# Up-projection of the channel mixer: block products chained in PSUM banks, three engines in a written-out order, GpSimd without elementwise work

## The chip, the cores and the metric

The kernel runs on one core of a Trainium2 chip. The metric is the device time of one launch in microseconds (us); the median of three runs is given. Engines: PE is TensorE (matmul), PEld its weight loads, DVE is VectorE, ACT is ScalarE, POOL is GpSimd, SP is SyncE, which here only issues DMAs.

## The reference, cut to what matters

Two layers of a decoder trunk (1024 tokens, 1024 channels, float32). Layer 0 mixes tokens by a short convolution and differential attention, layer 1 by RWKV-7. Behind each mixer stands the channel mixer, the only part that the change touches:

```python
def conv_glu_ffn(x, w_up, conv_w, conv_b, w_down):
    h = causal_dwconv(x @ w_up, conv_w) + conv_b     # 1024 -> 2 * 2816 columns; width-3 conv over tokens
    gate, up = jnp.split(h, 2, axis=-1)
    return (jax.nn.silu(gate) * up) @ w_down         # 2816 -> 1024
```

Products are float32 to nearly full precision: each operand is split into a high and a low part, and three matmuls (high by high, high by low, low by high) stand for one.

## The kernel before, in words

The up-projection takes the 5632 columns as 22 column tiles, c = 0 to 21; a tile is 128 gate columns and the 128 value columns that belong to them. As a 2 x 2 block product (columns by halves of the channels, times halves of the channels by halves of the tokens) a tile needs seven block products, by Winograd's form of Strassen's scheme. They are numbered 1 to 7 and written P1 to P7 below. Each is 4 x 3 = 12 matmuls of 128x128 by 128x512 (`mm3`, three lines in a row, called from `product`), so a tile is 84 matmuls.

Around the products of one tile stands elementwise work:

- Four sums of weight blocks, S1 to S4 (`block`, tile `ws`), on POOL in before. The weights `wr` come by two DMAs of 512 KB a tile (part 0 and part 1), issued by SP.
- For each product the split of its weight block (`prep`): a cast on ACT to the high part, a subtraction on DVE for the low part (both into tile `wu`), FLA = 5 products ahead.
- Sums of the products (`add`, on DVE, tiles `u`, `hv` and the PSUM tile `up`), and one copy on ACT.
- The convolution of the gate half and of the value half (`conv`): the first tap on ACT, the other two on DVE (tile `cv`), then SiLU on ACT and the product of gate and value, on POOL in before. The result `G` goes to DRAM by a DMA that POOL issues.

The generator `ffn` does one step for each product. Tiles 0 and 1 go side by side, product by product (14 steps); from then on (20 tiles, 140 steps) one tile follows the other. Their first steps run while the mixer's output projection ends, since the operands B11, B21, B22 and T1 to T4 (tiles `x`, `xt`) are made from the mixer's layer norm in `mixer_operands`; T3 and T4 are subtracted on POOL. `dn` is the down-projection that follows.

The order of each engine's queue is not the order of the code: the framework's scheduler sorts the instructions by priority and by its own estimate of times, and places semaphores. Each engine then takes its queue in order.

Of the kernel before, what the change touches and what calls it, by code (L numbers as in the profile page):

```python
# [13 lines left out]
ALU = mybir.AluOpType  # L14
# [16 lines left out]
FLA = 5  # L31
FILL = 3
# [31 lines left out]
class Kern:  # L64
# [73 lines left out]
    def mm3(self, ps, ah, al, bh, bl, first, last):  # L138
        nc = self.nc
        nc.tensor.matmul(ps, ah, bh, start=first, stop=False)  # L140
        nc.tensor.matmul(ps, ah, bl, start=False, stop=False)  # L141
        nc.tensor.matmul(ps, al, bh, start=False, stop=last)  # L142
# [41 lines left out]
    def mixer_operands(self, zs, half, gname, bname, xo):  # L184
        """the blocks B11, B21, B22 and sums T1 to T4 that the up-projection takes, in high and low parts"""
# [22 lines left out]
        for name, d, x, y in (("B22", None, None, None), ("T1", lo, (raw, lo), (old, lo)), ("T2", hi, (raw, hi), (ts, lo)),  # L208
                              ("T3", lo, (raw, hi), (raw, lo)), ("T4", hi, (ts, hi), (old, hi))):
# [8 lines left out]
    def ffn(self, l, xo, resid, tail, nxt=None):  # L218
        """generator, one step for each block product of the up-projection. That takes a gate tile and a value tile of
        128 columns together: as 2 x 2 blocks (columns by halves of the channels, times halves of the channels by  # L220
        halves of the tokens) they come from seven block products, by Winograd's form of Strassen's scheme."""
# [11 lines left out]
        def block(c, name):  # L233
            """a block of the weights, or a sum of such"""
# [17 lines left out]
        def prep(n):  # L252
            if n < len(seq):
# [3 lines left out]
                nc.scalar.copy(t[:, lo], src)  # L257
                nc.vector.tensor_sub(t[:, hi], src, t[:, lo].bitcast(F32))  # L258

        def conv(src, ct):  # L260
            cc = self.U("cv")
            nc.scalar.activation(cc, src, AF.Identity, bias=self.pc_(bname, ct), scale=self.pc_(wname, 88 + ct))  # L262
            nc.vector.scalar_tensor_tensor(cc[:, 1:], src[:, :T - 1], self.pc_(wname, 44 + ct), cc[:, 1:], ALU.mult, ALU.add)  # L263
            nc.vector.scalar_tensor_tensor(cc[:, 2:], src[:, :T - 2], self.pc_(wname, ct), cc[:, 2:], ALU.mult, ALU.add)  # L264
            return cc

        def product(c, i):
            w = W[c]
            xn = prods[i][1]
# [3 lines left out]
            t = w.pop(i)  # L273
            for j in range(4):
                k, x = j * P, xo[xn][j]
                self.mm3(ps, t[:, k:k + P], t[:, 512 + k:512 + k + P], x[:, lo], x[:, hi], j == 0, j == 3)
            add = nc.vector.tensor_add
# [7 lines left out]
            if i == 7:  # L285
# [4 lines left out]
                w["gate"] = True  # L290
            if i == 5:
                w["p5"] = ps
            if i in (3, 7) and "gate" in w and not any(k in w for k in (3, 7)):
                add(w["A"][:, hi], w["A"][:, hi], w["u"][:, hi])  # L294
                w["g"] = conv(w["A"], c)
                nc.scalar.activation(w["g"], w["g"], AF.Silu)
            if i == 4:
                nc.vector.tensor_sub(w["h"][:, lo], w["u"][:, lo], ps)
                v = conv(w["h"], NC + c)
                nc.gpsimd.tensor_tensor(v, w["g"], v, op=ALU.mult)  # L300
                nc.gpsimd.dma_start(GS[c], v)
                W[c].clear()
# [17 lines left out]
        for n, (c, i) in enumerate(seq):  # L320
            prep(n + FLA)
            product(c, i)
            if n == len(seq) - 3:
                operands(0, 0)
                operands(0, 1)
            yield
# [53 lines left out]
    def make_tail(self, gi, bi, row, mode):  # L380
        """gi, bi: parameter names; row: (g, b) DRAM rows. Returns (tail, result)."""
# [5 lines left out]
        def tail(t, r, dh):  # L387
            """goes on with half dh of a tile of tokens"""
# [50 lines left out]
    def out_proj(self, w, yhl, resid, tail, in_w=(0, 1, 7), eng=None):  # L439
        """generator: loads the weights, then goes on by tiles of 128 tokens"""  # L440
# [21 lines left out]
    def mixer0(self, then):  # L462
# [61 lines left out]
        # generators of filling work: each step is one half of a column tile of the input projection  # L524
# [51 lines left out]
        # attention, one tile of 128 queries of one head after the other  # L576
# [27 lines left out]
        def turn(hd, i, p):  # L604
            """the weights of one tile, keys first"""
# [54 lines left out]
        # operands of the output projection: the last head's come two tiles at a time  # L660
# [31 lines left out]
        # queries and keys of the first head follow the input as it arrives  # L692
# [68 lines left out]
    def rwkv(self, xf, then):  # L761
# [29 lines left out]
        def variant(i, kt, x=None, h=None, eng=None):  # L791
            """x plus its mixed difference to the token before: of all tokens, or of one half of them"""
# [8 lines left out]
        def ahead(items, make, n=2):  # L801
            """items with what make gives for them, n of these in the making before one is used"""
# [16 lines left out]
        def spread(xs, i, src=None):  # L819
            """generator: the operands of a projection"""  # L820
# [15 lines left out]
        def lora1(steps):  # L836
            """generator: the first products of several low-rank maps, over the channel tiles"""
# [104 lines left out]
        # receptance, with the loras between its tiles; its start fills the gap behind what comes before  # L942
# [33 lines left out]
        def gates():  # L976
            """generator: the gate, written out for later"""
# [28 lines left out]
        # second lora weights: high and low parts stacked against the doubled hidden rows  # L1006
# [605 lines left out]
```

## Time and profile before

| | us |
|---|---|
| median of three runs (lowest, highest) | 2854.09 (2852.14, 2866.19) |
| span of the profiled execution, the one time the page has for it | 2858.8 |
| PE busy, DVE busy, ACT busy, POOL busy | 2639.9, 2065.9, 1060.9, 850.0 |
| up-projection of layer 0: tiles 0 and 1, then tiles 2 to 21 | 537.9 to 603.2, 603.2 to 1010.3 |
| up-projection of layer 1: tiles 0 and 1, then tiles 2 to 21 | 2135.2 to 2198.2, 2198.2 to 2605.9 |

The stretches are read off the starts of the `up` matmuls: the 169th of a layer begins tile 2. The span is 4.7 us above the median run and lies between the lowest and the highest. Two things help in reading the rows. Instructions of one engine overlap a little in the records, so that what one costs is the distance to the next start, not its length. And a matmul's record is longer than its turn on PE for the same reason.

### The profile page before, as it was taken

What the parts mean: (1) busy time and instruction counts of PE and PEld (TensorE: products, weight loads), DVE (VectorE), ACT (ScalarE), POOL (GpSimd) and SP (SyncE); (2) the same over time, 40 slices, a digit from 0 to 9 for tenths busy, and PEclk for the clock granted to TensorE, in tenths of its full rate; (3) what the DMA queues carried; (4) which work ended last, traced back from release to release, by engine and by line L of the source; (5) the groups of instructions that cost most, each with busy time, mean ns of one, the idle gap of its engine ahead of it and who ended that gap; (6) DMA issues with size and microseconds to landing.
All of it is one profiled execution on the core that took longest, in us unless ns stands there. A gap on an engine that the chain in (4) does not pass through costs nothing. (4 is left out here: it accounts for less than half of the span.)

```text
span 2858.8 us, 38102 instructions
## 1 busy us (share of the span) xinstructions
PE 2639.9 (92%) x14736; PEld 2140.1 (75%) x14736; DVE 2065.9 (72%) x2796; ACT 1060.9 (37%) x1650; POOL 850.0 (30%) x558
## 2 busy tenths in 40 slices
PE   8999989979998999999998998688897999899998
PEld 6777777768777788777876777577776787778886
DVE  4645656699999964657778656777759999997463
ACT  3323343234343441526665223334224344334330
POOL 0000003564554303010045211345555455441000
PEclk9999979999999999999997998787998999999999
DMA  5111233122222173543256779777431222224751
GB/s 163 52 45 52 63 114 104 67 74 74 82 83 71 67 231 115 195 158 111 89 188 217 230 219 232 175 175 204 154 125 48 93 78 78 82 74 158 240 187 41
DMA packets 208678, 358.10 MB, mean 125 GB/s; under 512 B 88945, under 2 KB 118257, under 8 KB 208497
## 3 DMA queue, kind: packets, MB, share of 16 engines
q1 hardware_dynamic: 198704, 320.01, 36.1%
q0 software_dynamic: 9792, 35.66, 3.4%
q8 instruction: 116, 1.90, 0.3%
q14 instruction: 66, 0.53, 0.1%
HBM read 255.46 MB, written 95.94 MB: 123 GB/s over the span
## 5 line engine op out<-in xcount | busy, mean ns | idle before, releaser
L140 PE MATMUL up<-x,wu 128*128 128x512 f32 x1232 | 485.3, 397 | 47.4 <-DVE u L282 22.4
L142 PE MATMUL up<-x,wu 128*128 128x512 f32 x1232 | 479.0, 397 | 10.3 <-DVE wu L258 10.2
L141 PE MATMUL up<-x,wu 128*128 128x512 f32 x1232 | 486.1, 395 | 0.8 <-DVE x L148 0.7
L140 PEld LDWEIGHTS up<-x,wu 128*128 128x128 f32 x1232 | 234.5, 191 | 106.4 <-DVE up L284 26.7
L142 PEld LDWEIGHTS up<-x,wu 128*128 128x128 f32 x1232 | 234.7, 191 | 69.7 <-DVE wu L258 21.0
L300 POOL TENSOR_TENSOR cv<-cv,cv 128x1024 f32<-128x1024 f32 x44 | 161.3, 3665 | 413.5 <-DVE cv L264 362.6
L141 PE MATMUL dn<-wdl,gt 128*128 128x512 f32 x704 | 274.5, 390 | 0.7 <-DVE wdl L118 0.7
L140 PE MATMUL dn<-wdh,gt 128*128 128x512 f32 x704 | 273.9, 390 | 0.2 <-ACT xf L182 0.2
L141 PEld LDWEIGHTS up<-x,wu 128*128 128x128 f32 x1232 | 235.2, 191 | 51.2 <-DVE x L148 3.1
L142 PE MATMUL dn<-wdh,gt 128*128 128x512 f32 x704 | 271.2, 390 | 0.0
L258 DVE TENSOR_TENSOR wu<-wr,wu 128x512 fp32r<-128x512 f32 x132 | 223.8, 1716 | 6.4 <-ACT wu L257 6.4
L258 DVE TENSOR_TENSOR wu<-ws,wu 128x512 fp32r<-128x512 f32 x176 | 221.9, 1264 | 0.2 <-ACT wu L257 0.2
L118 DVE TENSOR_TENSOR wdl<-raw,wdh 128x1024 fp32r<-128x1024 f32 x88 | 116.5, 1324 | 100.6 <-ACT wdh L117 91.6
L262 ACT ACTIVATE cv<-up,par 128x1024 f32<-128x1024 f32 x44 | 53.1, 1207 | 363.1 <-DVE up L294 363.1
L141 PE MATMUL pr<-xv,wph 128*128 128x512 f32 x384 | 155.2, 404 | 6.1 <-DVE xv L816 4.2
L140 PE MATMUL pj<-x,wih 128*128 128x512 f32 x384 | 152.8, 408 | 7.7 <-ACT x L147 7.6
L140 PE MATMUL pr<-xv,wph 128*128 128x512 f32 x384 | 154.2, 406 | 5.8 <-DVE kp L1057 4.3
L142 PE MATMUL pr<-xv,wpl 128*128 128x512 f32 x384 | 155.2, 404 | 4.2 <-DVE wpl L118 4.2
L117 ACT CAST wdh<-raw 128x1024 fp32r<-128x1024 f32 x88 | 92.6, 1052 | 173.6 <-DMA raw<-wdn 108.7
L141 PEld LDWEIGHTS dn<-wdl,gt 128*128 128x128 f32 x704 | 132.5, 188 | 28.6 <-DVE wdl L118 1.1
L140 PEld LDWEIGHTS dn<-wdh,gt 128*128 128x128 f32 x704 | 132.6, 188 | 27.8 <-ACT xf L182 0.4
L142 PE MATMUL pj<-x,wil 128*128 128x512 f32 x384 | 153.2, 399 | 0.2 <-DVE wil L118 0.2
(301 smaller groups left out, 5700.6 us busy)
## 6 DMA issues: line engine op xcount, KB each, us to landing
wr<-wup SPq DMA_DIRECT2D x88, 512.0 KB, 3.6
raw<-wdn SPq DMA_DIRECT2D x88, 512.0 KB, 3.8
G<-cv POOLq DMA_DIRECT2D x44, 512.0 KB, 3.0
gr<-G SPq DMA_DIRECT2D x88, 256.0 KB, 3.8
bk<-bkS SPq DMA_DIRECT2D x32, 512.0 KB, 6.3
spill<-acc SPq DMA_DIRECT2D x24, 512.0 KB, 2.6
res<-spill SPq DMA_DIRECT2D x24, 512.0 KB, 4.8
raw<-win SPq DMA_DIRECT2D x22, 512.0 KB, 3.7
```

The source lines that it names most:

```text
L117: self.nc.scalar.copy(hi, raw)
L118: self.nc.vector.tensor_sub(lo, raw, hi.bitcast(F32))
L140: nc.tensor.matmul(ps, ah, bh, start=first, stop=False)
L141: nc.tensor.matmul(ps, ah, bl, start=False, stop=False)
L142: nc.tensor.matmul(ps, al, bh, start=False, stop=last)
L258: nc.vector.tensor_sub(t[:, hi], src, t[:, lo].bitcast(F32))
L262: nc.scalar.activation(cc, src, AF.Identity, bias=self.pc_(bname, ct), scale=self.pc_(wname, 88 + ct))
L300: nc.gpsimd.tensor_tensor(v, w["g"], v, op=ALU.mult)
```

## The change

From the 15th step of `ffn` on (tiles 2 to 21), in both layers:

- The queues of PE, DVE and ACT are no longer sorted by the scheduler: a region (`manual_schedule`) keeps them in the order of the code. A step (slot) issues its product's 12 matmuls, the subtraction for the product four slots on, its share of the convolution, one sum of blocks for the next tile, the cast for the product five slots on, and then the addition that takes this product. SP and POOL stay with the scheduler.
- Products are in the order 1, 6, 2, 5, 7, 3, 4 (before 1, 6, 5, 2, 7, 3, 4) and are chained in PSUM: P2 adds onto P1's bank, P5 and P3 onto P6's, P4 onto P7's. Before, each had a bank of its own, and DVE added. A tile has five additions on DVE in place of seven, and three banks (a two-bank tile `A`, and `z`) in place of one for each product.
- The four sums S1 to S4 and the product of gate and value move from POOL to DVE. POOL keeps the DMA of `G`.
- The convolution of a tile is spread over the slots of this tile and the next.

For tiles 0 and 1 the steps stay as they were, under the scheduler, but for the product of gate and value, which moves to DVE as well, and for T4, whose sign is turned so that its product is added instead of subtracted. Docstrings and some comments are dropped, which shifts line numbers: L258 of before is L265, L249 is L250, L300 is L301 and L352, and L140 to L142 are L141 to L143. The core of the diff:

```diff
-                nc.gpsimd.tensor_tensor(w[name], x, y, op=op)
+                (nc.vector if c > 1 else nc.gpsimd).tensor_tensor(w[name], x, y, op=op)
...
+        def tap(cc, src, ct, k):
+            if k == 0:
+                nc.scalar.activation(cc, src, AF.Identity, bias=..., scale=...)
+            else:
+                nc.vector.scalar_tensor_tensor(cc[:, k:], src[:, :T - k], ..., cc[:, k:], ALU.mult, ALU.add)
...
-                nc.gpsimd.tensor_tensor(v, w["g"], v, op=ALU.mult)
+            nc.vector.tensor_tensor(v, w["g"], v, op=ALU.mult)
...
+        def late(c, i):
+            b = c - 1
+            if i == 4:
+                w = W[c]
+                w["g"] = self.U("cv")
+                tap(w["g"], w["A"], c, 0)
+                tap(w["g"], w["A"], c, 1)
+            elif b > 1:
+                w = W[b]
+                if i == 1:
+                    w["v"] = self.U("cv")
+                    tap(w["v"], w["h"], NC + b, 0)
+                    tap(w["g"], w["A"], b, 2)
+                elif i == 6:
+                    nc.scalar.activation(w["g"], w["g"], AF.Silu)
+                    tap(w["v"], w["h"], NC + b, 1)
+                elif i == 2:
+                    tap(w["v"], w["h"], NC + b, 2)
+                elif i == 5:
+                    nc.vector.tensor_tensor(w["v"], w["g"], w["v"], op=ALU.mult)
+                    nc.gpsimd.dma_start(GS[b], w["v"])
+                    w.clear()
+            name = {1: "S1", 2: "S2", 7: "S3", 3: "S4"}.get(i)
+            if name and c + 1 < NC:
+                block(c + 1, name)
+
+        def chained(n, c, i):
+            w = W[c]
+            if i == 1:
+                w["A"], w["u"] = self.A("up"), self.U("u2")
+            if i == 7:
+                w["z"] = self.B("up")
+            if i == 6:
+                nc.scalar.copy(w["u"][:, lo], w["A"][:, lo])
+            ps = w["z"] if i in (7, 4) else w["A"][:, lo if i in (1, 2) else hi]
+            multiply(c, i, ps, i in (1, 6, 7), skip_group_check=True)
+            sub(n + FLA - 1)
+            late(c, i)
+            cast(n + FLA)
+            if i == 6:
+                add(w["u"][:, hi], w["u"][:, lo], ps)
+            if i == 5:
+                w["h"] = self.U("hv")
+                add(w["h"][:, hi], w["u"][:, lo], ps)
+            if i == 7:
+                add(w["h"][:, hi], w["h"][:, hi], ps)
+            if i == 3:
+                add(ps, ps, w["u"][:, lo])
+            if i == 4:
+                add(w["h"][:, lo], w["u"][:, hi], ps)
...
-        seq += [(c, i) for c in range(2, NC) for i in (1, 6, 5, 2, 7, 3, 4)]
+        seq += [(c, i) for c in range(2, NC) for i in (1, 6, 2, 5, 7, 3, 4)]
...
+                if n == 14:
+                    region.enter_context(self.tc.manual_schedule(engines=ORDERED))
+                if n < 14:
+                    prep(n + FLA)
+                    apart(c, i)
+                else:
+                    chained(n, c, i)
```

What stands in DVE's queue before, for a stretch a little over half a tile long in the middle of layer 0 (L258 the subtractions of the split, L282 to L298 the additions, L263 and L264 the taps; `wr` and `ws` name the source of a subtraction):

```order
L258 TENSOR_TENSOR wu_974_5497<-ws_973_5494,wu_974_5497 128x512
L284 TENSOR_TENSOR up_975_5500<-up_975_5500,u2_966_5455 128x512
L258 TENSOR_TENSOR wu_976_5514<-ws_973_5494,wu_976_5514 128x512
L287 TENSOR_TENSOR u2_966_5455<-u2_966_5455,up_977_5517 128x512
L258 TENSOR_TENSOR wu_979_5534<-wr_969_5474,wu_979_5534 128x512
L288 TENSOR_TENSOR hv_978_5530<-u2_966_5455,up_972_5481 128x512
L289 TENSOR_TENSOR u2_966_5455<-u2_966_5455,up_972_5481 128x512
L298 TENSOR_TENSOR hv_978_5530<-u2_966_5455,up_983_5560 128x512
L294 TENSOR_TENSOR up_975_5500<-up_975_5500,u2_966_5455 128x512
L263 SCALAR_TENSOR_TENSOR cv_980_5550<-up_975_5500,par_81,cv_980_5550 128x1023
L263 SCALAR_TENSOR_TENSOR cv_984_5574<-hv_978_5530,par_81,cv_984_5574 128x1023
L264 SCALAR_TENSOR_TENSOR cv_980_5550<-up_975_5500,par_81,cv_980_5550 128x1022
```

The same queue now, from the slot of P1 of a tile on (L265 the subtractions, L250 the sums S1 to S4, L277 the taps, L352 gate by value, L374 and L377 the additions that take P6 and P5):

```order
L265 TENSOR_TENSOR wu_894_5012<-ws_883_4947,wu_894_5012 128x512
L277 SCALAR_TENSOR_TENSOR cv_890_5003<-hv_881_4931,par_81,cv_890_5003 128x1023
L374 TENSOR_TENSOR u2_889_4989<-u2_889_4989,up_888_4988 128x512
L265 TENSOR_TENSOR wu_895_5030<-wr_875_4872,wu_895_5030 128x512
L277 SCALAR_TENSOR_TENSOR cv_890_5003<-hv_881_4931,par_81,cv_890_5003 128x1022
L250 TENSOR_TENSOR ws_893_5010<-ws_893_5010,wr_891_5006 128x512
L265 TENSOR_TENSOR wu_896_5048<-wr_891_5006,wu_896_5048 128x512
L352 TENSOR_TENSOR cv_890_5003<-cv_886_4982,cv_890_5003 128x1024
L377 TENSOR_TENSOR hv_898_5067<-u2_889_4989,up_888_4988 128x512
L265 TENSOR_TENSOR wu_897_5065<-ws_893_5010,wu_897_5065 128x512
L250 TENSOR_TENSOR ws_900_5083<-wr_891_5006,wr_892_5008 128x512
L379 TENSOR_TENSOR hv_898_5067<-hv_898_5067,up_899_5069 128x512
```

One subtraction now stands in each slot, taps and additions alternate with them, and the sums and the product of gate and value have come over from POOL.

On SP, the loads of the weights `wr` in the middle of layer 0, before (part 0 and part 1 of a tile, then those of the next):

```order
L239 DMA wr_948_5332<-wup 128x1024
L239 DMA wr_949_5334<-wup 128x1024
L239 DMA wr_969_5474<-wup 128x1024
L239 DMA wr_970_5476<-wup 128x1024
L239 DMA wr_990_5616<-wup 128x1024
```

and now (part 0 of tile 7, part 1 of tile 6, part 0 of tile 8, part 1 of tile 7, part 0 of tile 9):

```order
L240 DMA wr_908_5142<-wup 128x1024
L240 DMA wr_892_5008<-wup 128x1024
L240 DMA wr_925_5278<-wup 128x1024
L240 DMA wr_909_5144<-wup 128x1024
L240 DMA wr_942_5414<-wup 128x1024
```

Part 1 of a tile now stands behind part 0 of the tile after it. A part 0 waits until the tile two before has given its buffer back, which its S4 on DVE does last.

On PE, the seam between P6 and the next product of tile 2, before (each product its own bank, `up_842`, then `up_846`):

```order
L140 MATMUL up_842_4608<-x_791_4321,wu_823_4486 128x512
L141 MATMUL up_842_4608<-x_791_4321,wu_823_4486 128x512
L142 MATMUL up_842_4608<-x_791_4321,wu_823_4486 128x512
L140 MATMUL up_846_4629<-x_784_4293,wu_827_4512 128x512
L141 MATMUL up_846_4629<-x_784_4293,wu_827_4512 128x512
```

and now (P6, then P2; both write the two-bank tile `up_838`, each one half):

```order
L141 MATMUL up_838_4588<-x_791_4321,wu_823_4486 128x512
L142 MATMUL up_838_4588<-x_791_4321,wu_823_4486 128x512
L143 MATMUL up_838_4588<-x_791_4321,wu_823_4486 128x512
L141 MATMUL up_838_4588<-x_700_3781,wu_827_4512 128x512
L142 MATMUL up_838_4588<-x_700_3781,wu_827_4512 128x512
```

P2 now writes onto the bank that holds P1, so it waits for ACT's copy of P1; likewise P5 waits for the addition that reads P6, P3 for the one that reads P5, and P4 for the one that reads P7.

## Rows read from the trace of the kernel before

**Rows 1.** Page, part 1: busy us (share of the span) and instructions.
```profile
PE 2639.9 (92%) x14736; PEld 2140.1 (75%) x14736; DVE 2065.9 (72%) x2796; ACT 1060.9 (37%) x1650; POOL 850.0 (30%) x558
```

**Rows 2.** Windows of the up-projections: stretch, length, busy us by engine, TensorE clock, DMA.
```profile
537.90:603.20 65.30, 47.33 (x202) 37.88 (x201) 55.98 (x64) 27.42 (x45) 45.88 (x22) 0.87 0.16 57
603.20:1010.30 407.10, 391.19 (x1682) 315.57 (x1681) 380.64 (x364) 157.88 (x224) 193.81 (x118) 0.99 0.24 82
2135.20:2198.20 63.00, 48.44 (x202) 37.52 (x201) 58.84 (x64) 25.78 (x43) 38.99 (x20) 0.86 0.14 51
2198.20:2605.90 407.70, 391.34 (x1681) 316.00 (x1680) 380.89 (x363) 157.93 (x223) 193.05 (x118) 0.99 0.25 82
```

**Rows 3.** Timeline, PE: start, us, instruction; 21 steps lie between these.
```profile
702.14 0.39 PE L140 MATMUL up<-x,wu 128*128 128x512 f32 x1
...
706.90 0.39 PE L140 MATMUL up<-x,wu 128*128 128x512 f32 x1
```

**Rows 4.** Timeline, DVE, one tile of layer 0.
```profile
853.39 0.68 DVE L282 TENSOR_TENSOR u<-u,up 128x512 f32<-128x512 f32 x1
853.99 6.94 DVE L258 TENSOR_TENSOR wu<-wr,wu 128x512 fp32r<-128x512 f32 x2
860.85 1.75 DVE L258 TENSOR_TENSOR wu<-ws,wu 128x512 fp32r<-128x512 f32 x1
862.52 0.69 DVE L284 TENSOR_TENSOR up<-up,u 128x512 f32<-128x512 f32 x1
```

**Rows 5.** Timeline, POOL, the same stretch.
```profile
853.01 2.70 POOL L300 TENSOR_TENSOR cv<-cv,cv 128x1024 f32<-128x1024 f32 x1 [8.13 <-DVE cv L264]
...
856.62 1.30 POOL L249 TENSOR_TENSOR ws<-wr,wr 128x512 f32<-128x512 f32 x1
...
860.45 1.60 POOL L249 TENSOR_TENSOR ws<-ws,wr 128x512 f32<-128x512 f32 x1
```

**Rows 6.** Timeline, PE, the same stretch; the wait is in brackets.
```profile
858.27 0.39 PE L141 MATMUL up<-x,wu 128*128 128x512 f32 x1
863.26 0.80 PE L140 MATMUL up<-x,wu 128*128 128x512 f32 x1 [4.60 <-DVE up L284]
863.85 0.63 PE L141 MATMUL up<-x,wu 128*128 128x512 f32 x1
...
867.26 0.63 PE L140 MATMUL up<-x,wu 128*128 128x512 f32 x1
```

**Rows 7.** Groups of lines, 603.2 to 1010.3: busy us, mean ns.
```profile
L258 DVE TENSOR_TENSOR wu<-wr,wu 128x512 fp32r<-128x512 f32 x58 | 103.1, 1797 | 0.0
L258 DVE TENSOR_TENSOR wu<-ws,wu 128x512 fp32r<-128x512 f32 x78 | 96.5, 1237 | 0.0
L300 POOL TENSOR_TENSOR cv<-cv,cv 128x1024 f32<-128x1024 f32 x21 | 77.3, 3681 | 189.7 <-DVE cv L264 164.3 <-ACT cv L296 25.4
L262 ACT ACTIVATE cv<-up,par 128x1024 f32<-128x1024 f32 x20 | 24.1, 1207 | 181.2 <-DVE up L294 181.2
```

**Rows 8.** Timeline, DVE, while POOL stands still.
```profile
713.50 0.68 DVE L282 TENSOR_TENSOR u<-u,up 128x512 f32<-128x512 f32 x1
714.09 0.68 DVE L258 TENSOR_TENSOR wu<-ws,wu 128x512 fp32r<-128x512 f32 x1
714.69 1.28 DVE L264 SCALAR_TENSOR_TENSOR cv<-hv,par,cv 128x1022 f32<-128x1022 f32 x1
715.89 0.69 DVE L258 TENSOR_TENSOR wu<-ws,wu 128x512 fp32r<-128x512 f32 x1
```

**Rows 9.** Instructions of tile `wr`: the DMAs' time from issue to landing.
```profile
DMA to landing us min/median/max: 3.3/3.6/5.9
```

**Rows 10.** Timeline, PE, tiles 0 and 1 of layer 0: the longest wait.
```profile
589.95 0.77 PE L140 MATMUL up<-x,wu 128*128 128x512 f32 x1 [13.19 <-DVE u L282]
```

**Rows 11.** Timeline, DVE, the work before that wait's end.
```profile
584.12 5.09 DVE L148 TENSOR_TENSOR x<-xt,x 128x512 fp32r<-128x512 f32 x3
589.13 1.27 DVE L282 TENSOR_TENSOR u<-u,up 128x512 f32<-128x512 f32 x2
...
595.19 0.69 DVE L287 TENSOR_TENSOR u<-u,up 128x512 f32<-128x512 f32 x1 [2.47 <-PE up L142]
```

**Rows 12.** Timeline, POOL, the same stretch (L214 is T4; L249 the sums of tile 2).
```profile
578.61 6.72 POOL L214 TENSOR_TENSOR xt<-xt,xr 128x512 f32<-128x512 f32 x4
585.29 1.71 POOL L249 TENSOR_TENSOR ws<-wr 128x512 f32<-128x512 f32 x1
```

More of the change, by code (lines that the diff above doesn't have):

```diff
@@ L31 @@
 FLA = 5
+ORDERED = {mybir.EngineType.PE, mybir.EngineType.DVE, mybir.EngineType.Activation}
 FILL = 3
@@ L257, in prep, with sub, multiply, gate @@
                 nc.scalar.copy(t[:, lo], src)
-                nc.vector.tensor_sub(t[:, hi], src, t[:, lo].bitcast(F32))
+                casts[n] = src, t
+        def sub(n):
+            if n in casts and casts[n]:
+                src, t = casts[n]
+                casts[n] = None
+                nc.vector.tensor_sub(t[:, hi], src, t[:, lo].bitcast(F32))
+        def prep(n):
+            cast(n)
+            sub(n)
+        casts = {}
+        def tap(cc, src, ct, k):
+            if k == 0:
+                nc.scalar.activation(cc, src, AF.Identity, bias=self.pc_(bname, ct), scale=self.pc_(wname, 88 + ct))
+            else:
+                nc.vector.scalar_tensor_tensor(cc[:, k:], src[:, :T - k], self.pc_(wname, 88 - 44 * k + ct), cc[:, k:], ALU.mult, ALU.add)
         def conv(src, ct):
             cc = self.U("cv")
-            nc.scalar.activation(cc, src, AF.Identity, bias=self.pc_(bname, ct), scale=self.pc_(wname, 88 + ct))
-            nc.vector.scalar_tensor_tensor(cc[:, 1:], src[:, :T - 1], self.pc_(wname, 44 + ct), cc[:, 1:], ALU.mult, ALU.add)
-            nc.vector.scalar_tensor_tensor(cc[:, 2:], src[:, :T - 2], self.pc_(wname, ct), cc[:, 2:], ALU.mult, ALU.add)
-            return cc
-        def product(c, i):
-            w = W[c]
-            xn = prods[i][1]
+            for k in range(3):
+                tap(cc, src, ct, k)
+            return cc
+        def multiply(c, i, ps, first=True, **kw):
+            t, x = W[c].pop(i), xo[prods[i][1]]
+            for j in range(4):
+                k = j * P
+                self.mm3(ps, t[:, k:k + P], t[:, 512 + k:512 + k + P], x[j][:, lo], x[j][:, hi], first and j == 0, j == 3, **kw)
+        add = nc.vector.tensor_add
+        def gate(c):
+            w = W[c]
+            w["g"] = conv(w["A"], c)
+            nc.scalar.activation(w["g"], w["g"], AF.Silu)
+        def value(c):
+            w = W[c]
+            v = conv(w["h"], NC + c)
+            nc.vector.tensor_tensor(v, w["g"], v, op=ALU.mult)
+            nc.gpsimd.dma_start(GS[c], v)
+            w.clear()
+        def apart(c, i):
+            w = W[c]
             if i == 2:
@@ L272, in product @@
             ps = w["A"][:, lo] if i == 2 else w["A"][:, hi] if i == 3 else self.B("up")
[L273 to L277, printed above, removed]
+            multiply(c, i, ps)
             if i == 1:
@@ L289, in product @@
                 add(w["u"][:, hi], w["u"][:, hi], w["p5"])
-                w["gate"] = True
+                add(w["A"][:, hi], w["A"][:, hi], w["u"][:, hi])
+                gate(c)
             if i == 5:
                 w["p5"] = ps
[L293 to L296, printed above, removed]
             if i == 4:
-                nc.vector.tensor_sub(w["h"][:, lo], w["u"][:, lo], ps)
-                v = conv(w["h"], NC + c)
-                nc.gpsimd.tensor_tensor(v, w["g"], v, op=ALU.mult)
-                nc.gpsimd.dma_start(GS[c], v)
-                W[c].clear()
+                add(w["h"][:, lo], w["u"][:, lo], ps)
@@ new lines, in chained @@
+        def chained(n, c, i):
+            w = W[c]
+            if i == 1:
[20 more added lines that the diff above has]
+                add(w["h"][:, lo], w["u"][:, hi], ps)
@@ L318, in operands @@
                 dops[tg, c] = (self.split_half(r, "gt"),) + self.load_split(wdn[l, c], self.W if not tg and c < 3 else self.U, "wd")
[L320 to L326, printed above, removed]
+        with ExitStack() as region:
+            for n, (c, i) in enumerate(seq):
+                if n == 14:
[5 more added lines that the diff above has]
+                    chained(n, c, i)
+                if n == len(seq) - 3:
+                    operands(0, 0)
+                    operands(0, 1)
+                yield
+            for i in (1, 6, 2, 5):
+                late(NC, i)
         for tg in range(2):
```

18 lines of the change are left out of this document (11 added, 7 removed).

## Prediction

> **What bounds the kernel now.** I read the page's busy times first: PE is busy for 92% of the span, the next engine for 72% [rows 1]. What can be won is therefore PE's idle time and its time at half clock, and it has to be looked for where the change acts. The windows of the two up-projections show where [rows 2]. Tiles 2 to 21 take 407.1 us in layer 0 and 407.7 in layer 1 (814.8 together), which is 20.37 us for a tile. What a tile would take if PE never stood still comes from two starts of undisturbed matmuls: 4.76 us for 21 steps, or 0.2267 us a step [rows 3], so 84 matmuls take 19.04 us and 20 tiles 380.8. The two stretches thus lose 26.3 and 26.9 us. DVE is busy there for 380.6 of 407.1 us [rows 2]; the next question is whether it works or is held up.
>
> One tile shows it. Two subtractions of the split, alike in kind to one that takes 0.6 us elsewhere, fill 6.94 us, and the next takes 1.75 [rows 4]. In just this time POOL runs the product of gate and value and the four sums, from 853.01 to 862.05 [rows 5]. An addition stands behind them in DVE's queue at 862.52, and PE waits for it for 4.60 us; then nine steps take 4.00 us where 2.04 would do, at half the clock at first [rows 6]. Over the whole stretch the 136 subtractions take 103.1 + 96.5 = 199.6 us [rows 7], where 136 x 0.60 would be 82. The step of 0.60 us, and 1.20 for a tap of 1022 columns, is the distance between starts while POOL rests [rows 8]. So 118 us of DVE's time in a layer (5.9 a tile) is waiting behind POOL, and that is what makes DVE late.
>
> **The change part by part.**
>
> DVE's load. A tile has 7 subtractions, 5 additions and now 4 sums of 512 columns, and 4 taps and now one product of gate and value of 1024: 16 x 0.60 + 5 x 1.20 = 15.6 us. The sums and the product on DVE are not in the trace. The sums have the form of the subtractions, two operands in SBUF, so I take their 0.60; the product has the columns of a tap, 1.20. From below they can't be under zero, from above I bound them by the lengths in the records, 0.69 and 1.28 [rows 8]. Before, the tile cost 7 x 0.60 + 7 x 0.60 + 4 x 1.20 = 13.2 and the 5.9 of waiting. So DVE falls from 19.1 to 15.6 of PE's 19.04.
>
> Fixed order. Slots on PE are 19.04 / 7 = 2.72 us. DVE's slots hold 2.4 us (P1, P6, P2, P5, P4) or 1.8 (P7, P3), so none is over. I laid one tile out by hand, allowing 0.25 us from the end of a product to the addition that takes it, and counting from the end of P3. The addition behind P3 ends at 0.85. The first tap of the gate on ACT takes 1.2 us from there [rows 7], so the second tap on DVE can't begin before 2.2, 0.7 later than DVE is free: the only wait for another engine than PE. The addition behind P4 ends at 4.0, DVE's work in the slot of P1 at 6.4, the addition behind P6 at 9.0, the work of P2's slot at 11.4, the addition behind P5 at 14.45, that behind P7 at 17.2 and S4 at 18.4. So DVE is level with PE again before the tile is over. The waits that the change adds lie on PE: P2 for ACT's copy of P1, P5, P3 and P4 for the additions behind P6, P5 and P7. All of PE's queue waits behind each. PE comes to P5 at 10.9, to P3 at 16.3, to P4 at 19.0, each 1.8 us or more after its condition is met, so they cost nothing; if DVE's lag grows by more than 1.8 us, PE pays every us beyond. The first tap on ACT waits for DVE, and the casts wait behind it, but they serve products five slots on.
>
> Weights. On SP, part 1 of a tile's weights now stands behind part 0 of the next one's, and that waits for S4 of the tile two before. From S4 of one tile (18.4 - 19.04 = -0.6 in the layout) to S1 in the next (5.8), which needs part 1, there are 6.4 us. One load lands 3.3 to 5.9 us after issue, mostly 3.6 [rows 9]; two in a row I estimate at 5.5 to 6, from the one at 3.6 and a transfer of about two more. That is just in time: cost zero, at most half a us of DVE's slack.
>
> Seam from tile 1 to tile 2. This costs. Tiles 0 and 1 leave DVE a backlog: from the addition L287 (595.19 before [rows 11]) to the addition that reads P6 of tile 2, the queue now holds 19 instructions of 0.60 and 9 of 1.20, 22.2 us. P5 may not write before that is done. With the start moved 2.2 us earlier (next paragraph), DVE is there at 593.0 + 22.2 = 615.2. PE gets to P5 at 601.0 + 3 x 2.72 = 609.2. I charge 6.0 us, and 2.0 for the half clock behind it, as seen behind the wait of 4.60 [rows 6]. Bounds: 0 if the scheduler's backlog clears faster, 12 if it is doubled.
>
> T3 and T4 stay on POOL, and so does the long wait in tiles 0 and 1, 13.19 us for the addition L282 [rows 10]. But its end moves. Three subtractions before it take 5.09 us from 584.12 on, in place of 1.8, since POOL goes on to the sums of tile 2 at 585.29 [rows 11, 12]. With those on DVE, behind that point in its queue, the three can end at about 586.9, once T4 is through, and L282 starts 2.2 us earlier, and with it PE. Bounds 0 and 3.2. I take layer 1 for the same.
>
> End of the stage. DVE and ACT finish tile 21 in about 6 us while PE does the down-projection of tiles 0 and 1 (2.7 us each); the operands of the third are ready about half a us late, as the additions and taps before did it too. Zero, bounds -1 and +1. The scheduler also shifts the recurrence of layer 1 a little, where the diff has nothing; no more than some tens of matmuls trade places, so I take zero and keep 5 us on either side.
>
> Sum against the profiled execution: 20 tiles at 19.04 is 380.8, with the seam 388.8. Layer 0 gains 407.1 - 388.8 = 18.3, layer 1 18.9, the end of the long wait 2 x 2.2: 41.6 us in all. That execution's span is 4.7 us above the median run, 0.2%, which is too little to scale by. 2854.1 - 41.6 = 2812.
>
> One rule speaks against the slack. The Trainium skill, "VectorE: DVE Perf Modes", section Terms, has the pipeline emptied behind every operation before the next can issue. By it an instruction costs its length, not the distance of starts. But the rows have starts 0.60 apart at lengths of 0.68 [rows 8], so the measurement decides. By the rule a tile would need 16 x 0.68 + 5 x 1.28 = 17.3 us, still under 19.04, but the backlog at the seam would be 24.4, and the time 2817.
>
> **The rivals.**
>
> DVE becomes the bound. If each of its 21 instructions costs 0.2 us more than the starts show, because more of them now wait on a semaphore, a tile takes 15.6 + 4.2 = 19.8, and PE goes at that pace: 814.8 - (40 x 19.8 + 16) = 6.8 us gained, and 4.4: 2843. For it: the queue is in a fixed order and alternates with PE; the only slack is 3.4 us a tile. Against it: in [rows 8] neighbours with and without a wait stand at the same 0.60.
>
> The weights come late (slower). From S4 to S1 runs a loop through SP: load, then S1 to the next S4, which is 10.8 us of DVE's work. The tile's time is 10.8 plus the time of two loads, if that is over 19.04. It decides from 8.2 us on; from about 9.3 on the change is a loss. At 11 us: 40 x 21.8 + 16 - 814.8 - 4.4 = +69, or 2923. For it: the new order on SP. Against it: loads land in 5.9 us at the longest [rows 9], and DMA engines are busy for a quarter of the time [rows 2].
>
> The change doesn't do what it says. If POOL is not what holds DVE, the 5.9 us a tile stay, on top of 15.6 and the wait for ACT of 0.7: 22.2 a tile, 40 x 22.2 + 16 - 814.8 = +89, or 2943. Against it: each long subtraction in [rows 4] lies beside POOL's work in [rows 5].
>
> **How the numbers follow.** My forecast has 82 in 100, DVE as the bound 10, late weights 5, the last 3. The forecast's own range is 2799 (the seam costs 1.5 us a layer in place of 8) to 2824 (6 us more in each layer). The whole range, 2799 to 2836, reaches on to just under the second case and leaves out that case's middle and the two slower ones. A measurement of this kernel tells about 0.5%, or 14 us, from no change. Faster by more than that means below 2840: the forecast whole, and 2 of DVE's 10, makes 0.84. Within: the other 8. Slower: the last two, 0.08.
>
> **What would show it.** Right: no subtraction over 1 us in tiles 2 to 21, the stretch of a layer at 385 to 392 us, one wait of PE of 3 to 8 us at the third or fourth product of tile 2 and hardly any after it, DVE busy at 85% there, POOL only with DMAs. Wrong: a wait of PE for DVE in every tile (DVE the bound), S1 with a wait for a DMA in every tile (late weights), or long subtractions without POOL at work.

## The result, and the profile after

The changed kernel takes 2898.05 us, the median of four runs (2890.69 to 2912.32); the kernel before, in the same comparison, 2854.39. The ratio is 1.0149, with a 95% interval of 1.0114 to 1.0184: slower by 1.5%, where 2812 us was forecast. The profiled execution, the fastest of the four, has a span of 2888.9 us.

Part 1 of the page (answers [rows 1]):

```profile
PE 2632.4 (91%) x14736; PEld 2126.6 (74%) x14736; DVE 1956.9 (68%) x2920; ACT 1070.4 (37%) x1650; POOL 463.8 (16%) x354
```

The windows of the two up-projections, tiles 0 and 1 and then tiles 2 to 21, with the columns of [rows 2]:

```profile
533.45:598.49 65.04, 46.62 (x202) 37.08 (x200) 56.55 (x69) 29.32 (x47) 39.73 (x18) 0.90 0.18 65
598.49:1030.96 432.47, 397.25 (x1685) 315.29 (x1685) 321.99 (x421) 161.61 (x223) 11.42 (x21) 0.99 0.21 76
2142.14:2205.78 63.64, 47.09 (x201) 36.96 (x200) 58.24 (x69) 27.88 (x45) 35.12 (x16) 0.89 0.17 58
2205.78:2636.93 431.15, 396.06 (x1684) 314.20 (x1685) 322.01 (x421) 161.59 (x223) 11.29 (x21) 1.00 0.21 76
```

DVE fell from 381 to 322 us in a stretch and POOL from 194 to 11, as meant. The stretch itself grew by 25.4 and 23.4 us, at full clock. Between the two profiled executions the rest adds up to -18.7: 4.5 before tile 0 and 13.7 between the stretches went, tiles 0 and 1 changed by -0.3 and +0.6, the end by -0.9; together +30.1, the difference of the spans. The stretch between the layers, in which the diff edits nothing, ran from 1111 to 1126 us over the eleven profiles; what sets it stays open.

DVE's groups in 598.49 to 1030.96 (busy us, mean ns) answer [rows 7]:

```profile
L265 DVE TENSOR_TENSOR wu<-ws,wu 128x512 fp32r<-128x512 f32 x78 | 53.3, 684 | 0.0
L265 DVE TENSOR_TENSOR wu<-wr,wu 128x512 fp32r<-128x512 f32 x58 | 39.7, 684 | 0.0
```

No subtraction is long any more: 1797 and 1237 ns became 684. So DVE isn't held, and yet PE is later. One tile shows why. PE's timeline in tile 7, from the last matmul of P1 over P6 to the first steps of P2:

```profile
713.26 0.39 PE L143 MATMUL up<-x,wu 128*128 128x512 f32 x1
714.42 0.50 PE L141 MATMUL up<-x,wu 128*128 128x512 f32 x1 [0.77 <-ACT u L367]
714.75 0.39 PE L142 MATMUL up<-x,wu 128*128 128x512 f32 x1
...
717.06 0.39 PE L143 MATMUL up<-x,wu 128*128 128x512 f32 x1
718.30 0.50 PE L141 MATMUL up<-x,wu 128*128 128x512 f32 x1 [0.85 <-DVE u L374]
718.63 0.39 PE L142 MATMUL up<-x,wu 128*128 128x512 f32 x1
```

The two instructions it waits for, on ACT (the copy of P1) and on DVE (the addition that reads P6):

```profile
713.79 0.58 ACT L367 COPY u<-up 128x512 f32<-128x512 f32 x1
```

```profile
717.55 0.69 DVE L374 TENSOR_TENSOR u<-u,up 128x512 f32<-128x512 f32 x1 [1.27 <-PE up L143]
```

Neither is late: the copy starts 0.14 us after P1's last matmul ends (713.65), the addition 0.10 after P6's (717.45). PE stands still while they run, and goes on 0.05 and 0.06 us after their end. But P6 does not touch the bank that the copy reads, nor P2 the one that the addition reads: P1 and P2 write the first bank of tile `A`, P6 the second. Each product waits for the reader of the *other* bank. From start to start the two seams take 1.16 and 1.24 us where a step takes 0.2267 [rows 3]: 1.95 us lost, and the steps behind are a little slow (0.33 for the first). In sum a tile takes 21.28 us, 2.24 more than 84 undisturbed steps.

Over 640 to 1000, 17 tiles, the waits of PE (us in total, times, longest) are these two and no others:

```profile
PE up L141 <- DVE u L374: 14.4, 17, 0.9
PE up L141 <- ACT u L367: 13.1, 17, 0.8
```

The queue says the same without times. First matmuls of P1, P6, P2 and P3 of a tile in the changed kernel, with the engine whose semaphore they wait for (a semaphore is a counter that one engine raises and another waits on; names are cut to their last number):

```
3017 L141 MATMUL up_5532<-x_3772,wu_5456 128x512 [waits Activation_49]
3029 L141 MATMUL up_5532<-x_4309,wu_5473 128x512 [waits Activation_49]
3041 L141 MATMUL up_5532<-x_3781,wu_5493 128x512 [waits DVE_49]
3077 L141 MATMUL up_5532<-x_4280,wu_5556 128x512 [waits DVE_49]
```

All four write `up_5532`, one tile over two banks. P2 (3041) waits for DVE, and P5 behind it has no wait left of its own.

### The profile page after: what moved, and what is told of

It reads as the page before. It is cut to its first block, busy times and chain, and to the rows that moved or that the text cites. A ratio compares the mean times of both kernels' runs of the same rounds, so it can differ in the third digit from the quotient of the medians.

```text
span 2888.9 us, 37671 instructions
## 1 busy us (share of the span) xinstructions
PE 2632.4 (91%) x14736; PEld 2126.6 (74%) x14736; DVE 1956.9 (68%) x2920; ACT 1070.4 (37%) x1650; POOL 463.8 (16%) x354
## 5 line engine op out<-in xcount | busy, mean ns | idle before, releaser
L141 PE MATMUL up<-x,wu 128*128 128x512 f32 x1232 | 491.4, 401 | 99.1 <-DVE u L374 35.8
L142 PE MATMUL up<-x,wu 128*128 128x512 f32 x1232 | 484.6, 393 | 0.0
L143 PE MATMUL up<-x,wu 128*128 128x512 f32 x1232 | 483.5, 393 | 0.0
L141 PEld LDWEIGHTS up<-x,wu 128*128 128x128 f32 x1232 | 233.4, 190 | 181.6 <-DVE u L374 52.7
L142 PE MATMUL dn<-wdl,gt 128*128 128x512 f32 x704 | 274.5, 390 | 0.7 <-DVE wdl L119 0.7
L141 PE MATMUL dn<-wdh,gt 128*128 128x512 f32 x704 | 273.0, 391 | 0.2 <-ACT xf L183 0.2
L143 PE MATMUL dn<-wdh,gt 128*128 128x512 f32 x704 | 272.8, 390 | 0.0
L143 PEld LDWEIGHTS up<-x,wu 128*128 128x128 f32 x1232 | 233.6, 190 | 50.6
L142 PEld LDWEIGHTS up<-x,wu 128*128 128x128 f32 x1232 | 233.7, 190 | 47.6 <-DVE x L149 1.2
L258 ACT CAST wu<-ws 128x512 fp32r<-128x512 f32 x176 | 107.8, 615 | 242.2 <-PE up L143 229.5
L141 PE MATMUL pj<-x,wih 128*128 128x512 f32 x384 | 152.2, 407 | 7.6 <-ACT x L148 7.6
L142 PE MATMUL pr<-xv,wph 128*128 128x512 f32 x384 | 153.1, 399 | 5.2 <-DVE xv L905 3.8
L258 ACT CAST wu<-wr 128x512 fp32r<-128x512 f32 x132 | 80.8, 617 | 207.6 <-PE up L143 145.9
L141 PE MATMUL pr<-xv,wph 128*128 128x512 f32 x384 | 152.5, 402 | 5.6 <-DVE kp L1146 3.5
L143 PE MATMUL pr<-xv,wpl 128*128 128x512 f32 x384 | 153.5, 400 | 4.0 <-DVE wpl L119 4.0
L353 POOL DMA_DIRECT2D G<-cv x40 | 21.3, 532 | 835.9 <-DVE cv L352 835.9
L142 PE MATMUL pj<-x,wih 128*128 128x512 f32 x384 | 153.9, 401 | 0.0
L143 PE MATMUL pj<-x,wil 128*128 128x512 f32 x384 | 153.6, 400 | 0.2 <-DVE wil L119 0.2
L142 PEld LDWEIGHTS dn<-wdl,gt 128*128 128x128 f32 x704 | 132.6, 188 | 28.3 <-DVE wdl L119 1.1
L141 PEld LDWEIGHTS dn<-wdh,gt 128*128 128x128 f32 x704 | 132.6, 188 | 28.0 <-ACT xf L183 0.4
```

The source lines that it names most:

```text
L141: nc.tensor.matmul(ps, ah, bh, start=first, stop=False, **kw)
L142: nc.tensor.matmul(ps, ah, bl, start=False, stop=False, **kw)
L143: nc.tensor.matmul(ps, al, bh, start=False, stop=last, **kw)
L353: nc.gpsimd.dma_start(GS[b], w["v"])
```

## The experiments

Theory T says: the framework places semaphores by tile, not by bank; chaining put products that follow each other into two halves of one tile, so that each waits for the reader of the one just done. Rivals: the written-out order (R1), PE's own cost of chained banks (R2), the work that came to DVE (R3). Times of 20 tiles, in both layers, and of one tile in the middle:

| kernel | one tile, us | tiles 2 to 21, us | median, us | ratio to before (95%) |
|---|---|---|---|---|
| before | 19.0 to 28.4 | 407.1, 407.7 | 2854 to 2864 | 1 |
| after | 21.28 | 432.5, 431.2 | 2898.05 | 1.0149 (1.0114 to 1.0184) |
| e1 own bank | 19.04 | 384.2, 384.1 | 2809.6 | 0.9837 (0.9815 to 0.9859) |
| e2 before, sums and product on DVE | 19.04 | 380.8, 380.8 | 2799.22 | 0.9797 (0.9777 to 0.9816) |
| e3 after, sums on POOL | 21.29 | 431.4, 430.3 | 2908.2 | 1.0175 (1.0151 to 1.0198) |
| e4 after, scheduler's order | 22.17 | 447.3, 446.5 | 2929.31 | 1.0256 (1.0229 to 1.0282) |
| e5 own bank, sums on POOL | 19.04 | 383.5, 383.6 | 2811.05 | 0.9823 (0.9791 to 0.9855) |
| e6 before, P3 in an own bank | 20.54 | 409.2, 409.2 | 2864.6 | 1.0002 (0.9986 to 1.0018) |
| e7 own bank, scheduler's order | 19.17 | 390.6, 392.2 | 2821.37 | 0.986 (0.9826 to 0.9894) |
| e8 before, product on DVE | 19.1, every third 20.2 | 388.2, 388.1 | 2819.63 | 0.987 (0.9838 to 0.9902) |
| e9 before, sums on DVE | 19.04 | 381.9, 381.9 | 2800.22 | 0.979 (0.977 to 0.981) |

**e1: the second chain in a tile of its own.**

```diff
-            ps = w["z"] if i in (7, 4) else w["A"][:, lo if i in (1, 2) else hi]
+            if i == 6:
+                w["H"] = self.B("up")
+            ps = w["z"] if i in (7, 4) else w["A"][:, lo] if i in (1, 2) else w["H"]
...
-                add(ps, ps, w["u"][:, lo])
+                add(w["A"][:, hi], ps, w["u"][:, lo])
```

> The changed kernel, with the chain of P6, P5 and P3 in a one-bank tile H of its own; only the addition behind P3 still writes its result into the second bank of A. The arithmetic, the order of the queues and the number of instructions stay. Theory T (two halves of the two-bank tile A are guarded as one tile, so that P6 waits for ACT's copy of P1 and P2 for the addition that reads P6, though each reads the other bank): both waits of each tile go, a tile falls from 21.28 us to 19.04 to 19.2, the tiles 2 to 21 of a layer from 432 to 386 to 392 us, and the time to about 2812 (2800 to 2825). Rival R1 (the fixed order itself is late: DVE and ACT come to the copy and the addition too late for PE in any case): PE stands still at the next product that needs them, a tile stays at 21 us or more, 2890 to 2905. Rival R2 (alternating between chained banks costs PE by itself, no semaphore): tile unchanged at 21.3, 2898.

Measured: 2809.6 us, a tile 19.04, and no wait of PE at all from 640 to 960. Windows of tiles 2 to 21, columns as above:

```profile
598.79:982.95 384.16, 382.02 (x1683) 315.90 (x1684) 321.85 (x420) 161.45 (x223) 11.40 (x21) 1.00 0.24 85
2171.35:2555.48 384.13, 383.45 (x1683) 317.16 (x1684) 321.84 (x420) 161.44 (x223) 11.27 (x21) 1.00 0.24 85
```

The order, the chaining and DVE's load (322 us) are those of the changed kernel; only the tile of P6, P5 and P3 is another, and the addition behind P3 writes its sum over into `A`. T holds; R1 and R2 fall, as does R3: with 16.1 us a tile (321.85 / 20) DVE keeps up with PE. In the queue the first matmul of P2 waits for ACT alone now, and P5, which writes the bank that the addition reads, has the wait for DVE:

```
3041 L141 MATMUL up_5539<-x_3781,wu_5500 128x512 [waits Activation_49]
...
3053 L141 MATMUL up_5566<-x_4293,wu_5517 128x512 [waits DVE_49]
```

One might say that e1 merely has one more bank to turn in. The trace of the changed kernel speaks against it: what it names ahead of P6 is the copy of P1, from a bank that P6 does not use.

**e4 and e7: the scheduler's order, with the shared tile and with the own bank.** The edit in both:

```diff
-                if n == 14:
-                    region.enter_context(self.tc.manual_schedule(engines=ORDERED))
```

> The changed kernel without the region of fixed order: the scheduler sorts the queues of PE, DVE and ACT, the code and the chaining stay. Theory T (the waits come from the tile that two banks share, not from the order): waits of PE for ACT's copy and for DVE's addition remain, in other places, tile 20.3 to 22 us, 2860 to 2920. Rival R1 (the fixed order is the cost): the scheduler puts other matmuls before those that wait, tile 19.0 to 19.8, 2810 to 2840.

> The changed kernel with the own bank for P6, P5 and P3 and without the region of fixed order: the scheduler sorts PE, DVE and ACT. With the shared tile this order took 22.17 us a tile, with three waits of PE: for a cast, for ACT's copy, and for the addition behind P5 (which guards P3). Theory T (only the waits between products in one tile are false): the wait for ACT's copy goes, that of P3 for the addition behind P5 (one and the same bank, hence a true one) and that for the cast stay, a tile of 20.8 to 21.6 us, 2875 to 2905. Rival R1 (the scheduler, free of the false waits, finds an order without any): 19.0 to 19.3 us, 2805 to 2820.

Measured: 2929.31 and 2821.37. e4 has three waits of PE a tile (one tile's):

```profile
708.49 0.50 PE L141 MATMUL up<-x,wu 128*128 128x512 f32 x1 [0.78 <-DVE hv L377]
717.71 0.50 PE L141 MATMUL up<-x,wu 128*128 128x512 f32 x1 [0.75 <-ACT wu L258]
719.14 0.50 PE L141 MATMUL up<-x,wu 128*128 128x512 f32 x1 [0.70 <-ACT u L367]
```

That is 0.17 us a tile and 9 us in all over T's range for e4, with waits of the kind it names. For e7 I had expected that two of the three stay, as true waits. None stayed: from 640 to 960 PE waits for nothing, and R1's 19.0 to 19.3 came true, with an order sorted anew; its time is 1.4 us above R1's range. So the shared tile costs under either order, and without it the written-out order is worth 0.13 us a tile and a shorter end (the last tile takes 23.7 us in e7, 19.7 in e1). It is not what made the kernel slower.

**e3 and e5: the sums back on POOL, with the shared tile and with the own bank.** The edit in both:

```diff
-                (nc.vector if c > 1 else nc.gpsimd).tensor_tensor(w[name], x, y, op=op)
+                nc.gpsimd.tensor_tensor(w[name], x, y, op=op)
```

> The changed kernel, with the four sums of weight blocks put back on POOL; order, chaining and the product of gate and value on DVE stay. Theory T: POOL's sums hold DVE's subtractions again (4 to 7 us in a record), DVE's place in the fixed order slips by up to 4 us a tile, and the two waits of PE grow with it: a tile 21.5 to 23.5 us, 2905 to 2990. Rival R3 (the sums are a load on DVE that the fixed order can't carry): relieved of 2.4 us a tile, a tile gets shorter than 21.28, 2850 to 2895.

> The changed kernel with the own bank for P6, P5 and P3, and with the four sums of weight blocks back on POOL. It asks whether POOL's sums cost anything once the two waits are gone: with the shared tile, putting them back moved a tile by nothing (21.28 to 21.30). Theory P (in the fixed order DVE has so much slack that POOL's hold is hidden; what it cost before the change came through the scheduler's order, where the product of gate and value stood beside them): tile 19.04 to 19.3, time 2805 to 2825. Rival Q (the hold was hidden only behind the 2.2 us of PE's waits; without them it comes out): tile 19.8 to 21, time 2840 to 2890.

Measured: 2908.2 and 2811.05. In e3 the time is in T's range, but not for T's reason: a tile did not become longer (21.29), where 21.5 to 23.5 was expected. What e3 has more stands in tiles 0 and 1, 67.9 and 67.4 us in place of 65.0 and 63.6, and between the layers. R3, which wanted it shorter, is wrong as well. In e5 theory P holds: not a tenth of a us a tile. POOL does hold DVE there, as these rows of e5 show, POOL first:

```profile
701.17 1.31 POOL L250 TENSOR_TENSOR ws<-wr 128x512 f32<-128x512 f32 x1 [6.80 <-DMA wr<-wup]
702.56 1.63 POOL L250 TENSOR_TENSOR ws<-ws,wr 128x512 f32<-128x512 f32 x1
...
710.29 1.30 POOL L250 TENSOR_TENSOR ws<-wr,wr 128x512 f32<-128x512 f32 x1
711.55 1.28 POOL L250 TENSOR_TENSOR ws<-wr,ws 128x512 f32<-128x512 f32 x1
```

```profile
700.92 1.28 DVE L277 SCALAR_TENSOR_TENSOR cv<-up,par,cv 128x1022 f32<-128x1022 f32 x1
...
702.95 2.32 DVE L277 SCALAR_TENSOR_TENSOR cv<-hv,par,cv 128x1023 f32<-128x1023 f32 x1
...
710.75 2.64 DVE L265 TENSOR_TENSOR wu<-ws,wu 128x512 fp32r<-128x512 f32 x1
713.32 0.67 DVE L381 TENSOR_TENSOR hv<-hv,up 128x512 f32<-128x512 f32 x1
...
715.59 0.70 DVE L383 TENSOR_TENSOR up<-up,u 128x512 f32<-128x512 f32 x1 [0.99 <-PE up L143]
```

A tap of 1.28 us takes 2.32, a subtraction of 0.68 takes 2.64, and still DVE waits for PE at L383: the hold fits into its slack.

**e2, e8, e9: the kernel before, with POOL's work moved and nothing else.** e2 makes both edits, e8 the first alone, e9 the second alone:

```diff
-                nc.gpsimd.tensor_tensor(v, w["g"], v, op=ALU.mult)
+                nc.vector.tensor_tensor(v, w["g"], v, op=ALU.mult)
...
-                nc.gpsimd.tensor_tensor(w[name], x, y, op=op)
+                (nc.vector if c > 1 else nc.gpsimd).tensor_tensor(w[name], x, y, op=op)
```

> The kernel before, with one part of the change alone: the four sums of weight blocks of tiles 2 to 21 and the product of gate and value on DVE in place of POOL; the scheduler orders the queues, each product has its own bank. Theory T (POOL's elementwise work held DVE for 5.9 us a tile, and it is the new waits of the chaining that cost): subtractions of 0.7 us throughout, DVE 13.2 + 4 x 0.6 + 1.2 = 16.8 us a tile of 19.04, tile 19.1 to 20.0 us in place of 20.37, the time 2800 to 2845. Rival R3 (moving POOL's work to DVE is itself the loss, since DVE gets 3.6 us more a tile than it is relieved of): tile 21 us or more, over 2870.

> The kernel before, with only the product of gate and value on DVE; the four sums of weight blocks stay on POOL. Sums on POOL lengthened DVE's instructions by 3.4 us a tile where PE ran without a stop (subtractions of 1259 in place of 684 ns, taps of 2258 in place of 1276). Theory L (only DVE's load counts): 13.2 + 1.2 + 3.4 = 17.8 us of a tile's 19.04, so no wait of PE, tile 19.04 to 19.2, time 2798 to 2815. Rival M (sums that still hold DVE for several us at a stretch make PE wait at some product though the load fits): tile 19.5 to 20.2, 2820 to 2850.

> The kernel before, with only the four sums of weight blocks of tiles 2 to 21 on DVE; the product of gate and value stays on POOL. Theory L: 13.2 + 2.4 and what the product holds, 5.9 - 3.4 = 2.5, is 18.1 us of 19.04, so tile 19.04 to 19.2, time 2798 to 2815. Rival M (the product, 2.7 us long and more, holds DVE at one place just ahead of an addition that PE waits for): tile 19.5 to 20.4, 2820 to 2855.

Measured: 2799.22, 2819.63, 2800.22. The first is just under T's range and the shortest time of the study. In its stretch PE is busy from the first to the last matmul:

```profile
597.58:978.37 380.79, 380.79 (x1681) 315.42 (x1680) 341.98 (x463) 157.50 (x224) 11.40 (x21) 1.00 0.26 87
```

That is 26.3 us of 407.1 won in layer 0 and 26.9 in layer 1, all of PE's idle time there. e9 needs one edited line for nearly the same, as theory L has it. e8 lies just between L and M; its wait is this, once in three tiles, behind a subtraction that stands beside POOL's sums (PE, then DVE, then POOL):

```profile
716.59 0.47 PE L140 MATMUL up<-x,wu 128*128 128x512 f32 x1 [0.70 <-DVE u L287]
```

```profile
711.14 4.71 DVE L258 TENSOR_TENSOR wu<-ws,wu 128x512 fp32r<-128x512 f32 x1
715.77 0.67 DVE L287 TENSOR_TENSOR u<-u,up 128x512 f32<-128x512 f32 x1
```

```profile
711.51 1.30 POOL L249 TENSOR_TENSOR ws<-wr,wr 128x512 f32<-128x512 f32 x1
712.76 1.29 POOL L249 TENSOR_TENSOR ws<-wr,ws 128x512 f32<-128x512 f32 x1
714.01 1.28 POOL L249 TENSOR_TENSOR ws<-wr 128x512 f32<-128x512 f32 x1
```

So POOL's elementwise work was the whole loss of tiles 2 to 21 in the kernel before: moving the product alone wins 18.9 of layer 0's 26.3 us (407.1 - 388.2), the sums alone 25.2. The two don't add up: both win the same idle time of PE, and at 380.8 there is none left.

One thing more follows from e1 and e2, which were timed beside the same runs of the kernel before. e2 is the shorter by 10.4 us, without the fixed order and without the chaining. So on this record these two parts bring nothing beyond the move of POOL's work, not even with the own bank: e1 takes longer at the ends of the stretch (384.2 in place of 380.8 us, in tile 2 and the last tile) and in tiles 0 and 1 (65.3 and 65.8 in place of 62.8 and 61.8).

**e6: the shared tile in the kernel before.** There P2 and P3 share a tile, and PE's longest wait was P3's for L284, which reads P2 [rows 6].

```diff
-            ps = w["A"][:, lo] if i == 2 else w["A"][:, hi] if i == 3 else self.B("up")
+            ps = w["A"][:, lo] if i == 2 else w["A"][:, hi] if i == 3 and c < 2 else self.B("up")
+            if i == 3:
+                w["p3"] = ps
...
-                add(w["A"][:, hi], w["A"][:, hi], w["u"][:, hi])
+                add(w["A"][:, hi], w["p3"], w["u"][:, hi])
```

> The kernel before, with P3 of tiles 2 to 21 in a one-bank tile of its own, so that it no longer waits for the addition behind P2 (L284), which reads and writes the other bank of the tile that P2 and P3 shared. POOL keeps its work. Theory T2 (the kernel before paid for a shared tile too: without it PE would run ahead of the late DVE): a tile falls from 20.37 us to 19.1 to 19.7, time 2805 to 2835. Rival (DVE is late on average there, not only at this one wait, so PE only waits one or two products further on): 20.1 to 20.5 a tile, 2845 to 2862, and the long wait is named by another addition.

Measured: 2864.6 and 20.46 us a tile on average, no change, as the rival has it (the time is 2.6 us above its range). From 640 to 970 PE now waits for another addition instead:

```profile
PE up L140 <- DVE u L289: 17.3, 14, 1.3
```

There P7 stands between P2 and P3, so that the false wait is met early unless DVE is late; and where DVE is late, PE waits at another product anyway.

## Why the prediction was wrong, by its own steps

- **What bounds the kernel: right.** POOL's work held DVE, and DVE's lateness was PE's idle time. The forecast had 18.3 and 18.9 us a layer for the whole change; the move alone (e2) brings 26.3 and 26.9.
- **DVE's load: right in size.** 15.6 us a tile were worked out; the records, with overlaps counted once, give 16.1. The sums take 681 to 688 ns, the product 1218, inside the bounds. The Trainium skill ("VectorE: DVE Perf Modes", section Terms) says that the next operation can't issue until the pipeline is empty. The prediction read this as a start that waits for the whole length of the record before it; L374 of tile 7 is 0.69 us long, and the next starts 0.61 behind it (718.16), so by the measurement, as in [rows 8], it doesn't. When the pipeline is empty no row shows.
- **Fixed order: this step failed.** "The waits that the change adds lie on PE: P2 for ACT's copy of P1, P5, P3 and P4 for the additions behind P6, P5 and P7", each met 1.8 us or more ahead. That is the list by banks, which stands at the end of "The change" too. As such it holds: in e1 PE waits nowhere from 640 to 960. But the semaphores of the changed kernel go by tile `A`, and so P6 waits for the copy of P1 and P2 for the addition behind P6, each directly behind the product that feeds it, so that nothing can hide them: 0.93 + 1.01 us start to start, 2.24 with the slow steps behind. The step cost 0 in the sum and 43.7 and 42.4 us a layer in the trace (432.5 and 431.2 against the forecast 388.8; 19 tiles at 2.24 are 42.6, the rest is the seam and the end). That 2812 and these 86 make just the 2898 that was measured is luck. The profiled execution grew by 30.1 us where it was to lose 41.6; of these 71.7 us, 86 come from the two stretches and -14 from the rest, mostly from the -13.7 between the layers. The own bank (e1) takes the two waits away, and the time is 2809.6. That this is near the forecast 2812 is in part luck too, since terms below were mis-sized both ways.
- **Weights: right.** From 598 to 1031 no wait of DVE is for a DMA; the landing of `wr` (640 to 1000) is as in [rows 9]:

```profile
DMA to landing us min/median/max: 3.4/3.7/5.2
```

- **Seam from tile 1 to tile 2: mechanism right, split and mis-sized.** 8 us were charged, as one wait of P5. Tile 2 takes 27.13 and 25.56 us, 8.1 and 6.5 over; that this is near 8 is luck, for it comes from the two waits of every tile in a longer form. PE in layer 0, the first matmuls of P1, P6 and P2 of tile 2:

```profile
598.49 0.47 PE L141 MATMUL up<-x,wu 128*128 128x512 f32 x1 [2.39 <-DVE cv L277]
...
604.00 0.80 PE L141 MATMUL up<-x,wu 128*128 128x512 f32 x1 [2.50 <-ACT u L367]
...
610.29 0.61 PE L141 MATMUL up<-x,wu 128*128 128x512 f32 x1 [1.84 <-DVE u L374]
```

  DVE's backlog was sized well: from the first addition L321 of that round (587.96, L287 of before) to L374 (609.56) 21.6 us, and 22.2 with L374 itself, as forecast. With the own bank the wait stands at P5, as forecast, but takes 2.14 in place of 6.0 us, and tile 2 is 2.7 over. The first row says where the rest is: P1 now writes a tile of pool `A`, which tile 0 gives back only with its last tap, and waits 2.39 us for it. I had missed that wait.
- **The end of the long wait: right in layer 0, but given back; wrong in layer 1.** In layer 0 the subtractions before it take 2.95 us where they took 5.09 [rows 11], and the wait 11.10 where it was 13.19 [rows 10]. PE, DVE and POOL (T4 alone now, no sums behind it):

```profile
583.45 0.76 PE L141 MATMUL up<-x,wu 128*128 128x512 f32 x1 [11.10 <-DVE u L316]
```

```profile
579.75 2.95 DVE L149 TENSOR_TENSOR x<-xt,x 128x512 fp32r<-128x512 f32 x3
```

```profile
574.24 6.71 POOL L215 TENSOR_TENSOR xt<-xr,xt 128x512 f32<-128x512 f32 x4
```

  The 2.1 us are lost again at the wait of 2.39 just named: tiles 0 and 1 take 65.0 against 65.3. In e2, where P1 has a bank of its own, they take 62.8. Layer 1 was taken for the same, but there the three subtractions took 1.88 us already, so that nothing was to be won at them, and the wait became longer (DVE and PE of before, then PE of the changed kernel):

```profile
2183.16 1.88 DVE L148 TENSOR_TENSOR x<-xt,x 128x512 fp32r<-128x512 f32 x3
```

```profile
2185.78 0.76 PE L140 MATMUL up<-x,wu 128*128 128x512 f32 x1 [9.19 <-DVE u L282]
```

```profile
2190.40 0.76 PE L141 MATMUL up<-x,wu 128*128 128x512 f32 x1 [9.75 <-DVE u L316]
```

  In e2 it is 7.07, so the move of the sums won 2.1 us there too; what took them away in the changed kernel stays open.
- **End of the stage, and what lies between the layers.** The first was in its bounds: the last tile of a layer takes 0.9 us more than its neighbours in the changed kernel, and 0.7 in e1. For the second, zero and 5 us on either side were kept, and the profiled executions differ by 13.7. Executions of the kernel before alone lie up to 21 us apart (2849.5 to 2870.24 in one comparison), so one pair can't say whether the change did it.
- **The rivals.** None was the case, although the sign that was to show DVE as the bound, a wait of PE for DVE in every tile, is in the trace. It misleads: DVE is busy for 322 of 432 us and starts its addition only when PE has ended P6. "DVE becomes the bound" and "the weights come late" are refuted by e1, and "POOL is not what holds DVE" by e9. A rival by which a wait is guarded by tile was missing, though [rows 6] held the sign of it: P3 waiting for L284, which reads the other bank.

## What to carry to other kernels

Read an added wait off the tile that the framework guards, and not off the bank or the bytes: two chains that alternate need a tile each, else a product can wait for the reader of the one just before it. A wait of PE for an instruction that starts only when the product just ended is a full round trip, and no slack of the engine covers it; look for it in the queue with its semaphores before summing up. Where one edit removes a cause and others come with it, time it alone first: one line of this change (e9) brought 2.1%, and the whole lost 1.5%.

## What the runs showed of the hardware

- Rotating through banks was not enough. The Trainium skill ("Perfetto Trace Analysis", section Matmuls) asks that independent groups of matmuls go through different banks, so that the reading of one overlaps the next. P1 and P6 of the changed kernel do go to different banks, yet P6 starts only when the reading of P1 has ended (two such waits a tile); in e1 nothing waits, at 19.04 us a tile. What holds P6 is the framework's semaphore, not the bank; the rule holds here for banks that are tiles of their own.
- Beside POOL's sums not all of DVE's work gets longer. In e5 the first of the taps that read `hv` and `cv`, both in SBUF, goes from 1276 to 2258 ns in the mean, the subtractions that read `ws` from 684 to 1259. Those that read `wr` never stand beside a sum there, and keep their 678. The tap that reads `up`, in PSUM, takes its 1.28 us at 700.92, though a sum runs beside it from 701.17 on. The Trainium skill ("SBUF — State Buffer", section "SBUF: two separate sides") has an exclusive lock between GpSimd and a DVE instruction with two SBUF inputs, where the GpSimd operation reads SBUF as well; these rows agree.
- At tile 2 of the changed kernel PE stood still for 2.39 us, did 12 matmuls, stood still for 2.50, and the next steps take 0.43 us; the granted clock is 0.62 over 604.0 to 608.1, between the levels of 1.2 and 2.4 GHz. In e1 36 matmuls lie between the waits of 2.40 and 2.14 us, and the steps behind take 0.24, at a granted clock of 1.00 (606 to 612). Behind the two short waits of each tile the clock is at 1.00 (680 to 700).
